# RMSNorm with SiLU on one core: three of four Squares on ScalarE, Silu by whole blocks, and constants and gamma's copy made in small pieces

## The chip, the core and the metric

The kernel runs on one core of a Trainium2 chip. The metric is the device time of one execution in microseconds (us). A single core has no second state to tell apart here: all executions but one (in e6) count as fast, and all have a granted clock of 1.0. The times of experiments are given as a ratio to the kernel before, run in the same rounds on the same chip, with a 95% interval. A ratio is the record's own figure, from fast runs of the same rounds, so it is not quite the ratio of the medians that are quoted, nor of the means of all listed runs. The span of a trace is about 1.8 us shorter than the device time of the same execution (316.25 against 318.03 for the profiled run of before).

## The reference

```python
x: (8, 1024, 2048) float32, gamma: (2048,), eps = 1e-5
rms = sqrt(mean(x**2, axis=-1, keepdims=True) + eps)
out = gamma * x / rms
return out * (1 / (1 + exp(-out)))          # SiLU
```

67.1 MB are read and 67.1 MB written, with a handful of operations on each element.

## The kernel before

The 8192 rows are cut into 16 blocks of 128 partitions by 4 rows (4 MB each). Six blocks are in flight. A block is loaded by SyncE's queue; its four sums of squares are split between VectorE and ScalarE; VectorE scales it by 1/rms and gamma; ScalarE does Silu in place and issues the store. The next load into the buffer waits for that store.

```python
def sums(b, after_first=()):
    na = J // 2                                  # J = 4 rows
    for j in range(na, J):
        nc.vector.tensor_tensor_reduce(out=junk_v, in0=row(b, j), in1=row(b, j), ..., accum_out=ss[:, j:j + 1])
    for j in range(na):
        nc.scalar.activation(out=junk_a, in_=row(b, j), func=ACT.Square, accum_out=ss[:, j:j + 1])
        if j == 0:
            for s in after_first:
                store(s)                         # store of an older block, issued behind the first Square
    ...                                          # Sqrt on ScalarE gives rms
def finish(b, halves=False):
    for j in range(J):
        nc.vector.scalar_tensor_tensor(...)      # row * rstd * gamma
        if j % 2:
            ...                                  # Silu on two rows at a time
...
        nc.vector.memset(ones, 1.0)              # 128 x 128
        ...                                      # gamma is spread by matmul with ones into PSUM
        nc.vector.tensor_copy(out=g, in_=junk_v) # 128 x 2048
        ...
        for b in range(1, last - 1):
            sums(b + 1, after_first=[b - 1])
            finish(b)
            invert(b + 1)
```

So the store of block b-1 stands on ScalarE's queue behind the first Square of block b+1, and with it behind the landing of load b+1.

## Time and profile before

| | before |
|---|---|
| device time, median of 6 | 317.48 us (317.27 to 317.81) |
| span of the profiled run | 316.3 us |
| bytes moved by DMA | 134.2 MB, 424 GB/s over the span |
| busy, VectorE and ScalarE | 71% and 71% |
| first store issued | 36.67 us |
| last half store issued / landed | 304.8 / 315.3 us |

The profile's main lines and how to read them are in the prediction below. Two views of it became important only afterwards. The first is the end of the run in 1 us windows (columns: window, length, busy time of PE, PEld, DVE, ACT, POOL with counts, PE clock, share of the 16 DMA engines, GB/s):

```profile
312.00:313.00 1.00, 0.00 (x0) 0.00 (x0) 0.00 (x0) 0.00 (x0) 0.00 (x0) 1.00 1.03 442
313.00:314.00 1.00, 0.00 (x0) 0.00 (x0) 0.00 (x0) 0.00 (x0) 0.00 (x0) 1.00 0.24 98
314.00:315.00 1.00, 0.00 (x0) 0.00 (x0) 0.00 (x0) 0.00 (x0) 0.00 (x0) 1.00 0.04 16
315.00:316.00 1.00, 0.00 (x0) 0.00 (x0) 0.00 (x0) 0.00 (x0) 0.00 (x0) 1.00 0.00 0
```

One DMA engine of 16 is a share of 0.0625. So the 16 engines do not finish together: most are done soon after 313, and one or two work on to 314.9. The second is in the page's list of DMA queues, with packets, MB and share of 16 engines' span:

```profile
q1 hardware_dynamic: 2304, 67.11, 49.7%
...
q14 instruction: 3, 0.02, 0.0%
```

Queue q1 carries the loads. Queue q14 carries the program itself: three packets of 8192 bytes in this run.

### The profile page before, as it was taken

What the parts mean: (1) busy time and instruction counts of PE and PEld (TensorE: products, weight loads), DVE (VectorE), ACT (ScalarE), POOL (GpSimd) and SP (SyncE); (2) the same over time, 40 slices, a digit from 0 to 9 for tenths busy, and PEclk for the clock granted to TensorE, in tenths of its full rate; (3) what the DMA queues carried; (4) which work ended last, traced back from release to release, by engine and by line L of the source; (5) the groups of instructions that cost most, each with busy time, mean ns of one, the idle gap of its engine ahead of it and who ended that gap; (6) DMA issues with size and microseconds to landing.
All of it is one profiled execution on the core that took longest, in us unless ns stands there. A gap on an engine that the chain in (4) does not pass through costs nothing.

```text
span 316.3 us, 444 instructions
## 1 busy us (share of the span) xinstructions
PE 2.1 (1%) x8; PEld 0.5 (0%) x8; DVE 223.5 (71%) x147; ACT 223.8 (71%) x144; POOL 0.2 (0%) x4
## 2 busy tenths in 40 slices
PE   0200000000000000000000000000000000000000
PEld 0000000000000000000000000000000000000000
DVE  0679499999493983939849397593966939993900
ACT  1357958999967777678676687676786776879540
POOL 0000000000000000000000000000000000000000
DMA  8999999999999999999999999999999999999996
GB/s 328 402 464 410 452 390 410 452 419 443 439 424 452 411 452 410 452 414 456 406 456 414 448 414 448 439 423 452 414 452 410 452 414 456 406 456 410 452 407 269
DMA packets 4763, 134.25 MB, mean 425 GB/s; under 512 B 532, under 2 KB 532, under 8 KB 536
## 3 DMA queue, kind: packets, MB, share of 16 engines
q1 hardware_dynamic: 2304, 67.11, 49.7%
q10 hardware_dynamic: 2456, 67.12, 49.2%
q14 instruction: 3, 0.02, 0.0%
HBM read 67.12 MB, written 67.11 MB: 424 GB/s over the span
## 4 chain that ended last, share of the span: by engine, by line
DMA 74%; DVE 14%; ACT 5%; issue 2%; DVEq 1%; ACTq 0%; SPq 0%
DMA xt<-in_x_dram 44%; DMA out_dram<-xt 30%; DVE xt L84 11%; ACT xt L88 3%; DVE junk_v L64 3%; ACT junk_a L68 1%; DVEq L164 1%; ACT L74 0%; ACT rms L74 0%; DVE rstd L79 0%; ACTq L93 0%; DVE ss L64 0%; SPq L52 0%; DVEq L64 0%; ACTq L74 0%
## 5 line engine op out<-in xcount | busy, mean ns | idle before, releaser
L84 DVE SCALAR_TENSOR_TENSOR xt<-xt,rstd,g 128x2048 f32<-128x2048 f32 x64 | 146.2, 2347 | 0.1
L88 ACT ACTIVATE xt<-xt 128x4096 f32<-128x4096 f32 x32 | 115.4, 3615 | 36.8 <-DVE xt L84 36.7
L64 DVE CUSTOM_DVE_ANT_0 junk_v<-xt 128x2048 f32<-128x2048 f32 x32 | 73.5, 2298 | 56.1 <-DMA xt<-in_x_dram 55.5
L68 ACT ACTIVATE junk_a<-xt 128x2048 f32<-128x2048 f32 x32 | 60.1, 1879 | 29.2 <-DMA xt<-in_x_dram 28.3
L74 ACT ACT_TABLE_LOAD x15 | 19.2, 1283 | 9.9 <-DVE ss L64 9.9
L88 ACT ACT_TABLE_LOAD x15 | 19.2, 1283 | 3.1 <-DVE xt L84 2.9
L79 DVE RECIPROCAL rstd<-rms 128x4 f32<-128x4 f32 x16 | 2.8, 172 | 11.3 <-ACT rms L74 11.3
L114 DVE COPY g<-junk_v 128x2048 f32<-128x2048 f32 x1 | 2.3, 2292 | 9.2 <-PE junk_v L112 9.2
L68 ACT ACTIVATION_READ_ACCUMULATOR junk_a<-xt 128x1 f32 x32 | 6.0, 186 | 0.0
L74 ACT ACTIVATE rms<-ss,eps_t 128x4 f32<-128x4 f32 x16 | 4.8, 297 | 1.2 <-DVE ss L64 1.1
L64 DVE DVE_READ_ACCUMULATOR2_ANT ss<- 128x1 f32 x32 | 4.5, 141 | 0.0
L112 PE MATMUL junk_v<-xt,ones 1*128 1x512 f32 x8 | 2.1, 1133 | 8.1 <-DMA xt<-in_gamma_dram 8.1
L107 ACT ACT_TABLE_LOAD x1 | 1.3, 1283 | 0.7 <-PEq L150 0.7
L105 DVE MEMSET ones<- 128x128 f32 x1 | 0.2, 165 | 0.8 <-PEq L150 0.8
L112 PEld LDWEIGHTS junk_v<-xt,ones 1*128 1x128 f32 x8 | 0.5, 306 | 8.1 <-issue 8.1
L107 ACT ACTIVATE junk_a<-ones 128x1 f32<-128x1 f32 x1 | 0.2, 174 | 0.0
L150 POOL MEMSET const-uint8-127<- 128x1 uint8 x1 | 0.1, 102 | 0.0
L150 POOL MEMSET const-bfloat16-1.0<- 128x1 bf16 x1 | 0.1, 101 | 0.0
L150 POOL MEMSET const-float32-0.0<- 128x1 f32 x1 | 0.1, 98 | 0.2 <-issue 0.2
L150 POOL MEMSET const-float32-1.0<- 128x1 f32 x1 | 0.1, 98 | 0.0
L106 DVE MEMSET eps_t<- 128x1 f32 x1 | 0.1, 59 | 0.0
## 6 DMA issues: line engine op xcount, KB each, us to landing
xt<-in_x_dram SPq DMA_DIRECT2D x16, 4096.0 KB, 42.0
out_dram<-xt ACTq DMA_DIRECT2D x15, 4096.0 KB, 35.2
out_dram<-xt ACTq DMA_DIRECT2D x2, 2048.0 KB, 10.4
xt<-in_gamma_dram ACTq DMA_DIRECT2D x1, 8.0 KB
```

Of the source, the lines that this page charges most:

```text
L64: nc.vector.tensor_tensor_reduce(out=junk_v, in0=row(b, j), in1=row(b, j), scale=1.0, scalar=0.0, op0=ALU.mult, op1=ALU.add, accum_out=ss[ ...
L68: nc.scalar.activation(out=junk_a, in_=row(b, j), func=ACT.Square, accum_out=ss[:, j:j + 1])
L74: nc.scalar.activation(out=rms, in_=ss, func=ACT.Sqrt, scale=1.0 / d, bias=eps_t)
L79: nc.vector.reciprocal(out=rstd, in_=rmss.pop(b))
L84: nc.vector.scalar_tensor_tensor(out=row(b, j), in0=row(b, j), scalar=rstds[b][:, j:j + 1], in1=g, op0=ALU.mult, op1=ALU.mult)
L88: nc.scalar.activation(out=blocks[b][:, cols], in_=blocks[b][:, cols], func=ACT.Silu)
L105: nc.vector.memset(ones, 1.0)
L107: nc.scalar.activation(out=junk_a[:, 0:1], in_=ones[:, 0:1], func=ACT.Square)
L112: nc.tensor.matmul(junk_v[:, c * w:(c + 1) * w], ones[k:k + 1, :], grow[k:k + 1, 0:w], start=True, stop=True)
L114: nc.vector.tensor_copy(out=g, in_=junk_v)
L150: nc = _bacc.Bacc("TRN2", target_bir_lowering=False, num_devices=1)
L164: with _tile.TileContext(nc) as tc:
```

## The change

ScalarE squares three of four rows in blocks 2 to 14, so that VectorE, which waits for loads, sums one row; Silu runs once over a whole block (but for the last one), which saves ScalarE instructions. VectorE's constants and gamma's copy are made in 32 + 16 pieces instead of 1 + 1 instructions, 46 instructions more.

```diff
-        na = J // 2
+        na = J - 1 if 2 <= b <= 14 else J // 2
...
-            if j % 2:
-                cols = slice((j - 1) * d, (j + 1) * d)
+            if j % 2 and (halves or j == J - 1):
+                cols = slice((j - 1) * d, (j + 1) * d) if halves else slice(0, J * d)
...
-        nc.vector.memset(ones, 1.0)
+        for c in range(0, P, 4):
+            nc.vector.memset(ones[:, c:c + 4], 1.0)
...
-        nc.vector.tensor_copy(out=g, in_=junk_v)
+        for c in range(0, d, P):
+            nc.vector.tensor_copy(out=g[:, c:c + P], in_=junk_v[:, c:c + P])
```

## The prediction

> **What bounds the kernel now.** I read the page first: the busy tenths in 40 slices, the DMA total and the chain that ended last.
>
> ```profile
> ACT  1357958999967777678676687676786776879540
> DMA  8999999999999999999999999999999999999996
> HBM read 67.12 MB, written 67.11 MB: 424 GB/s over the span
> DMA 74%; DVE 14%; ACT 5%; issue 2%; DVEq 1%; ACTq 0%; SPq 0%
> ```
>
> The reader is to see that the transfers are at nine tenths or more in 38 of 40 slices, while VectorE and ScalarE are busy 71% of the span each, and that three quarters of the chain are transfers. The bytes are fixed: 134.2 MB. Then the groups by line, which price every instruction that the change touches:
>
> ```profile
> L84 DVE SCALAR_TENSOR_TENSOR xt<-xt,rstd,g 128x2048 f32<-128x2048 f32 x64 | 146.2, 2347 | 0.1
> L88 ACT ACTIVATE xt<-xt 128x4096 f32<-128x4096 f32 x32 | 115.4, 3615 | 36.8 <-DVE xt L84 36.7
> L64 DVE CUSTOM_DVE_ANT_0 junk_v<-xt 128x2048 f32<-128x2048 f32 x32 | 73.5, 2298 | 56.1 <-DMA xt<-in_x_dram 55.5
> L68 ACT ACTIVATE junk_a<-xt 128x2048 f32<-128x2048 f32 x32 | 60.1, 1879 | 29.2 <-DMA xt<-in_x_dram 28.3
> L114 DVE COPY g<-junk_v 128x2048 f32<-128x2048 f32 x1 | 2.3, 2292 | 9.2 <-PE junk_v L112 9.2
> L105 DVE MEMSET ones<- 128x128 f32 x1 | 0.2, 165 | 0.8 <-PEq L150 0.8
> ```
>
> Both engines wait for loads of x (55.5 us and 28.3 us). ScalarE's other wait, 36.7 us, is Silu waiting for VectorE's scaling. Third, the timeline of one steady block (columns: start, us, engine, line, what, then the idle time before it and its releaser):
>
> ```profile
> 84.02 1.88 ACT L68 ACTIVATE junk_a<-xt 128x2048 f32<-128x2048 f32 x1 [0.29 <-DMA xt<-in_x_dram]
> ...
> 88.74 9.13 DVE L84 SCALAR_TENSOR_TENSOR xt<-xt,rstd,g 128x2048 f32<-128x2048 f32 x4
> ...
> 97.91 3.62 ACT L88 ACTIVATE xt<-xt 128x4096 f32<-128x4096 f32 x1 [0.91 <-DVE xt L84]
> 103.39 1.88 ACT L68 ACTIVATE junk_a<-xt 128x2048 f32<-128x2048 f32 x1 [1.86 <-DMA xt<-in_x_dram]
> 103.45 0.34 ACTq L93 DMA_DIRECT2D out_dram<-xt  x1
> ```
>
> A load lands at 84.0; VectorE sums two rows, scales the block before it until 97.9; Silu's second half ends at 101.5; the next load lands 1.86 us later, and only then, behind the first Square of the new block, is the store issued. So per block the compute chain takes 17.5 us of a period of 19.4 us. (From 142.73 to 258.88 us there are six periods of 19.36 us: 8.39 MB in 19.36 us is 433 GB/s.) Fourth, the table of 4 us windows over the end; the last two columns are the DMA share and GB/s:
>
> ```profile
> 300.00:304.00 4.00, 0.00 (x0) 0.00 (x0) 1.09 (x1) 3.09 (x2) 0.00 (x0) 1.00 0.89 385
> 304.00:308.00 4.00, 0.00 (x0) 0.00 (x0) 0.00 (x0) 0.74 (x1) 0.00 (x0) 1.00 1.01 432
> 308.00:312.00 4.00, 0.00 (x0) 0.00 (x0) 0.00 (x0) 0.00 (x0) 0.00 (x0) 1.00 0.99 422
> 312.00:316.00 4.00, 0.00 (x0) 0.00 (x0) 0.00 (x0) 0.00 (x0) 0.00 (x0) 1.00 0.33 139
> ```
>
> Even in the tail the transfers do not run dry: the last two half stores are issued at 300.25 and 304.77, and data flows until about 313.3 (a third of the last window). The chain view puts VectorE and ScalarE on the path there, but the queue still held older stores.
>
> **What the Trainium skill says.** "DMA: Bandwidth & Descriptors", section Where 436 GB/s comes from, gives a ceiling of 435 GB/s for the 16 DMA engines of a core; 433 GB/s in the steady part agrees, so nothing is left to gain there. The same page, section Queues, rings and completion order, says that each DMA engine goes round the queues that have work. The windows agree as far as they go: with loads alone (4 to 36 us) the mean is 428 GB/s, and in the stores-only 304 to 312 us it is 427. So it matters whether any queue has bytes, not which. "ScalarE: Activation LUTs", section What ACT_TABLE_LOAD costs, gives 186 ns plus 0.833 ns an element, and 1283 ns a table load; the trace has 3617 ns for 4096 elements (the formula says 3598) and 1283 ns. "VectorE: DVE Perf Modes", section The TRN2 errata, says that many small pieces pay a fixed cost each, 120 cycles at 0.96 GHz when the source is PSUM; the trace before has no such piece.
>
> **The change part by part.** *Square.* For blocks 2 to 14, 13 row sums go from VectorE to ScalarE. From the timeline, one more Square with its accumulator read costs ScalarE 2.03 us (84.02 to 86.05), and one row sum fewer saves VectorE 2.39 us (84.13 to 86.52). Over the run this is +26 us on ScalarE and -31 us on VectorE.
>
> *Silu by blocks.* One 8192-element Silu is, from 3617 ns for 4096 and 0.833 ns for each further element, 7.03 us; two halves back to back take 7.12. It removes 15 instructions but only 0.1 us a block. What it costs is latency: Silu starts after the fourth scaled row, not the second.
>
> *Steady block.* New chain from a load's landing: 0.11 to VectorE's start, 2.39 for one row sum, 9.14 for four scalings, 0.03 handoff, 7.03 Silu: 18.7 us instead of 17.5. The period set by the transfers is 19.36 us, so 0.7 us of slack is left out of 1.86. ScalarE's own work per block is 3 x 2.03 + 1.28 + 0.30 + 1.28 + 7.03 = 16.0 us with its gaps, VectorE's 2.4 + 9.1 + 0.2 = 11.7: both below 19.36. Steady cost: zero.
>
> *Constants.* 32 memsets of 4 columns: the memset of one column took 59 ns, so about 32 x 60 ns = 1.9 us, from 0.8 to 2.8 us. ScalarE's warm-up reads column 0 alone, and dependencies here go by regions (before, the first Silu half starts after two of four rows), so gamma's load, issued at 1.03, keeps its place. The matmuls need all pieces, but start at 8.1. Cost zero.
>
> *Gamma's copy.* One copy took 2.29 us, from 10.24 to 12.5. A piece of 128 columns is 133 ns of data plus, by the skill's figure, 125 ns: 16 x 258 ns = 4.1 us (an estimate from that page), so it ends at about 14.4. VectorE's first row sum began at 13.24 when load 0 had landed: block 0 starts 1.1 us late.
>
> *Start-up.* Block 0's scaling then ends at 30.2, the whole Silu at 37.2 (before 32.7), the two Squares of block 1 at 41.2: store 0 is issued at 41.3 instead of 36.67. Until the backlog of landed loads is worked off, ScalarE is the bound at 16.0 us a block where the kernel before needed 14 (55.81, 69.78, 84.08). Stepping on: store 1 at 61.6 (was 55.8), store 2 at 77.6 (69.8), store 3 at 93.6 (84.1), store 4 at 109.6 (103.4), and then it catches up, since 16.0 is below 19.4. Does the DMA run dry? By 41.3 some 16.8 MB have moved, of 25.2 MB of loads issued. By 77.6 some 33 MB, of 37.7 issued even before store 2. By 109.6 some 47 MB, of about 54. There are always 4 MB or more queued, so delays of 5 to 10 us in issuing are absorbed. Cost zero.
>
> *Tail.* From the landing of load 14 (258.88): store 13 at +18.7 (was +17.5), store 14 at +28.0 (was +26.8), and all that follows 1.2 us later, so the last stores go out at 301.4 and 306.0. From 304.77 to 313.3 the DMA moved about 3.66 MB, of which 2.10 are the last half store: 1.56 MB, or 3.6 us, were queued ahead. A delay of 1.2 us is under that. At 300.25 it is 1.4 MB, or 3.3 us. Cost zero, with 2 us in reserve.
>
> **Sum:** 0 to 0.3 us; I predict 317.6 us.
>
> **Rivals.** (a) *ScalarE becomes the bound.* For it: Silu ends only 0.7 us before the next load, and ScalarE's busy share goes from 71% to about 79%. Against it: 16.0 us of work in 19.36, and VectorE need not wait for ScalarE to begin on a landed block. A load 1 us early would delay one store by less than 1 us, and two stores and two loads are in flight at a time (35 and 42 us to landing at 19.4 us a block). At worst the chain paced every block; even 1 us over on 12 blocks would give 329, but 18.7 does not reach 19.36. (b) *The tail runs dry.* If the start-up lag never closes, or the loads land later by s, the last store is late by 1.2 + s. Beyond 3.3 us each microsecond adds one: a lag of 5 us would give about 320. For it: stores 2 and 3 are 8 to 10 us late. Against it: late stores leave the DMA to the loads, so loads land earlier, not later. (c) *Gain:* VectorE loses 31 us of work and ScalarE 15 instructions. Where computing bound, it would show; here VectorE's saved 2.4 us a block only shortens a part of a chain that the longer Silu lengthens again. With the bytes fixed I see at most 0.5 us: 317. (d) The small pieces delay the start: at most 2 us, in front of a queue of 12 MB of loads; hidden.
>
> **Range and chances.** Fixed bytes at the ceiling hold the bottom at about 316.5. The top is rival (b) in a mild form, or a slightly different mix of loads and stores: 319.5. More than 2% faster (below 311.0) would need more than the DMA ceiling: 0.01. More than 2% slower (above 323.7) needs rival (a) or a large (b): 0.05. Within 2%: 0.94.
>
> **What would show it.** After the change I expect DMA at nine tenths in all but the end slices; 8192-element Silus of about 7.03 us; DVE busy down by about 28 us to 196 and ACT up by about 25 to 249; the copies of gamma lasting 3 to 4.2 us in all; the first store at about 41 us; in steady state idle time on ScalarE before the first Square of about 0.7 us, still released by the load; the last store at about 306. It would be wrong if the steady period grew, if windows below 390 GB/s appeared in the middle or before the last stores, or if stores were released by ScalarE throughout rather than by landed loads.

## The result

| | before | after |
|---|---|---|
| median of 6 | 317.48 us (317.27 to 317.81) | 318.92 us (317.79 to 319.30) |
| ratio of fast runs | | 1.0042 (1.0026 to 1.0059) |
| first store issued | 36.67 us | 40.47 us |
| last half store issued | 304.77 us | 303.76 us |
| last half store landed | 315.3 us | 316.6 us |

The issue of the first store in the two timelines, before and after:

```profile
36.67 0.36 ACTq L93 DMA_DIRECT2D out_dram<-xt  x1
40.47 0.36 ACTq L94 DMA_DIRECT2D out_dram<-xt  x1
```

About 1.3 us slower: within 2%, inside the range, above the 317.6 us foretold. The page of the changed kernel (busy tenths in 40 slices, the instruction queue, the bytes, the chain by engine):

```profile
ACT  1352994999999999997896868968689786797620
DMA  8999999999999999999999999999999999999994
...
q14 instruction: 4, 0.03, 0.0%
HBM read 67.12 MB, written 67.11 MB: 423 GB/s over the span
DMA 49%; ACT 22%; DVE 17%; issue 7%; DVEq 1%; PE 1%; ACTq 0%; SPq 0%
```

The DMA is as full as before. The chain now follows ScalarE through the start-up, which it did not before, but that is only the backlog described in the prediction: no transfer waits for it. The groups by line:

```profile
L85 DVE SCALAR_TENSOR_TENSOR xt<-xt,rstd,g 128x2048 f32<-128x2048 f32 x64 | 146.2, 2348 | 0.1
L69 ACT ACTIVATE junk_a<-xt 128x2048 f32<-128x2048 f32 x45 | 84.5, 1878 | 18.3 <-DMA xt<-in_x_dram 16.7
L65 DVE CUSTOM_DVE_ANT_0 junk_v<-xt 128x2048 f32<-128x2048 f32 x19 | 43.7, 2298 | 60.9 <-DMA xt<-in_x_dram 60.8
L117 DVE COPY g<-junk_v 128x128 f32<-128x128 f32 x16 | 3.3, 281 | 8.6 <-PE junk_v L114 8.6
L107 DVE MEMSET ones<- 128x4 f32 x32 | 0.9, 62 | 0.8 <-PEq L153 0.8
```

The 13 moved Squares, the unchanged scaling and the 48 pieces are all there; their durations are compared with the prediction below. A steady block in the timeline:

```profile
159.09 1.88 ACT L69 ACTIVATE junk_a<-xt 128x2048 f32<-128x2048 f32 x1 [0.91 <-DMA xt<-in_x_dram]
...
161.41 9.13 DVE L85 SCALAR_TENSOR_TENSOR xt<-xt,rstd,g 128x2048 f32<-128x2048 f32 x4
...
170.58 7.03 ACT L89 ACTIVATE xt<-xt 128x8192 f32<-128x8192 f32 x1 [2.51 <-DVE xt L85]
178.58 1.88 ACT L69 ACTIVATE junk_a<-xt 128x2048 f32<-128x2048 f32 x1 [0.97 <-DMA xt<-in_x_dram]
178.64 0.34 ACTq L94 DMA_DIRECT2D out_dram<-xt  x1
```

Period 19.5 us, Silu done at 177.61, and ScalarE still waits 0.97 us for the load, which also releases the store. So nothing is lost in the steady part. Nor in the last stores, which were issued 1.0 us *earlier* than before. Yet the last one landed 1.3 us later. The 1 us windows of the changed kernel's end show where:

```profile
313.00:314.00 1.00, 0.00 (x0) 0.00 (x0) 0.00 (x0) 0.00 (x0) 0.00 (x0) 1.00 0.39 164
314.00:315.00 1.00, 0.00 (x0) 0.00 (x0) 0.00 (x0) 0.00 (x0) 0.00 (x0) 1.00 0.08 33
315.00:316.00 1.00, 0.00 (x0) 0.00 (x0) 0.00 (x0) 0.00 (x0) 0.00 (x0) 1.00 0.04 16
```

The bulk ends within half a microsecond of before, and then a share of one engine in 16 works on for two microseconds. The trace holds, for each transfer, 16 completion marks, taken here as one for each DMA engine. Those of the last half store, on the clock of the span (the expectations below quote the trace's own clock, which is 11.1 us ahead):

```
             1st      15th     16th
before     313.46    314.46   315.33 us
after      313.70    314.65   316.59 us
```

Fifteen engines are 0.2 us later than before, the sixteenth 1.3 us. **The whole loss is one straggling DMA engine.** It was late early on: of the second load, the sixteenth mark came 0.85 us after the fifteenth, where before it was 0.15. Between these two loads lies the one thing that was not there before, an instruction packet at 17.4 us. The times of the instruction packets after the start are 93.6, 108.7 and 304.7 us in the kernel before, and 17.4, 98.0, 289.6 and 296.1 us after.

### The profile page after: what moved, and what is told of

It reads as the page before. It is cut to its first block, busy times and chain, and to the rows that moved or that the text cites. A ratio compares the mean times of both kernels' runs of the same rounds, so it can differ in the third digit from the quotient of the medians.

```text
span 317.5 us, 484 instructions
## 1 busy us (share of the span) xinstructions
PE 2.1 (1%) x8; PEld 0.5 (0%) x8; DVE 195.0 (61%) x167; ACT 246.6 (78%) x155; POOL 0.2 (0%) x4
## 3 DMA queue, kind: packets, MB, share of 16 engines
q1 hardware_dynamic: 2304, 67.11, 49.5%
## 4 chain that ended last, share of the span: by engine, by line
DMA 49%; ACT 22%; DVE 17%; issue 7%; DVEq 1%; PE 1%; ACTq 0%; SPq 0%
DMA out_dram<-xt 24%; DMA xt<-in_x_dram 23%; ACT xt L89 14%; DVE xt L85 13%; ACT junk_a L69 4%; DMA xt<-in_gamma_dram 2%; DVE junk_v L65 2%; ACT L75 2%; ACT L89 1%; DVE g L117 1%; DVEq L167 1%; PE junk_v L114 1%; ACT rms L75 0%; DVE rstd L80 0%; DVE ss L65 0%
## 5 line engine op out<-in xcount | busy, mean ns | idle before, releaser
L89 ACT ACTIVATE xt<-xt 128x8192 f32<-128x8192 f32 (+1 forms) x17 | 112.7, 6628 | 36.1 <-DVE xt L85 36.0
L69 ACT ACTIVATE junk_a<-xt 128x2048 f32<-128x2048 f32 x45 | 84.5, 1878 | 18.3 <-DMA xt<-in_x_dram 16.7
L65 DVE CUSTOM_DVE_ANT_0 junk_v<-xt 128x2048 f32<-128x2048 f32 x19 | 43.7, 2298 | 60.9 <-DMA xt<-in_x_dram 60.8
L117 DVE COPY g<-junk_v 128x128 f32<-128x128 f32 x16 | 3.3, 281 | 8.6 <-PE junk_v L114 8.6
L69 ACT ACTIVATION_READ_ACCUMULATOR junk_a<-xt 128x1 f32 x45 | 8.4, 186 | 0.0
L65 DVE DVE_READ_ACCUMULATOR2_ANT ss<- 128x1 f32 x19 | 2.7, 142 | 0.0
L107 DVE MEMSET ones<- 128x4 f32 x32 | 0.9, 62 | 0.8 <-PEq L153 0.8
```

Of the source, the lines that this page charges most:

```text
L89: nc.scalar.activation(out=blocks[b][:, cols], in_=blocks[b][:, cols], func=ACT.Silu)
L107: nc.vector.memset(ones[:, c:c + 4], 1.0)
L117: nc.vector.tensor_copy(out=g[:, c:c + P], in_=junk_v[:, c:c + P])
```

## The experiments

Two things were read from the traces of all runs besides the views above. *Fetches* are the instruction packets after the start. *Slow loads* are load packets of 32 KB begun after 50 us that took over 1240 ns, where nearly all take 1213; the figure behind them is their extra time summed over the 16 engines (16 us of it is 1 us of every engine). Packets carry no engine's number, but each engine's packets follow one another within some 5 ns, so they can be sorted into 16 chains; where two chains are in step the sorting is ambiguous. (The 241 slow packets and 72 us that the expectation of e4 quotes for e2 count from 41 us on; 216 of them begin after 50 us.) One profiled execution each:

```
                    first store   slow loads      last store's marks        fetches
                    issued        n, extra us     1st     15th    16th      (us)
before              36.7            2,  0.8      313.46  314.46  315.33     93.6 108.7 304.7
changed kernel      40.5            4,  0.6      313.70  314.65  316.59     17.4 98.0 289.6 296.1
e1_pieces           37.1            2,  0.8      313.33  314.66  315.44     18.4 95.4 264.6 304.1
e2_square_silu      40.0          216, 58.6      315.36  319.47  319.47     96.7 126.6 290.8
e3_pool_pad         37.0            8,  2.7      315.46  316.22  318.70     11 of them
e4_work_half0       36.5           14,  3.7      313.30  314.96  315.03     92.8 128.3 282.2
e5_whole0           40.0          170, 38.5      315.10  318.86  319.30     94.0 104.6 305.5
e6_after_half0      37.1            1,  0.2      313.63  315.13  315.31     18.4 95.6 281.3 297.2
e7_store0_late      40.1          211, 65.0      316.43  319.63  319.64     89.3 104.5 305.6
e8_store0_43        43.3            2,  0.8      313.40  314.37  315.20     89.9 103.8 298.6
e9_work_memsets     39.9          174, 51.1      315.65  318.61  319.06     52.1 97.3 293.0
e10_work_copies     40.4           13,  2.7      313.60  315.03  315.96     88.2 97.9 288.3
e11_pool_memsets    40.4           37,  5.5      313.49  314.93  316.60     88.2 97.8 289.4
```

The first theory, F: the fetch of VectorE's instructions takes turns with the data on one DMA engine, that engine never catches up, and the pieces bring such a fetch forward and add another. Its rival, W: the loss is in the work, the late stores of the start-up and the longer Silu.

### e0: the changed kernel again

No edit.

> The changed kernel once more, as the base for the others. In its trace one of the 16 DMA engines ended about 2.5 us after the other 15 (landings of the last store: fifteenth at 325.78, sixteenth at 327.72 on the trace's clock; kernel before 325.59 and 326.45). All theories: +1.0 to +1.6 us against before, and the same late last landing.

Median 318.94 us (318.12 to 319.32), ratio 1.0043 (1.0031 to 1.0055). Its fetches came at 17.7, 97.7, 288.1 and 294.9 us, and its last marks were 313.37, 314.40 and 316.61: the same straggler. Its first store went out at 40.78 us and its trace has no slow load (as defined above) at all, so this loss does not need slow loads.

### e1: the small pieces alone

```diff
 (kernel before)
-        nc.vector.memset(ones, 1.0)
+        for c in range(0, P, 4): nc.vector.memset(ones[:, c:c + 4], 1.0)
-        nc.vector.tensor_copy(out=g, in_=junk_v)
+        for c in range(0, d, P): nc.vector.tensor_copy(out=g[:, c:c + P], in_=junk_v[:, c:c + P])
```

> The kernel before with the 47 small pieces alone. Theory F (fetch): the loss is a DMA engine that fetches VectorE's instructions, 0.3 us of packet and up to 0.9 us in all each time; the 46 extra instructions bring its first fetch from 108.7 to about 17 us and add one near the end. Then this kernel loses most of the 1.3 us: +0.8 to +1.5 us, the instruction queue shows 4 packets or more, and the last landing is again 1.5 us or more after the fifteenth. Rival W (work): the loss is the late stores of the start-up and the longer Silu; then this kernel is within 0.3 us of before.

Median 319.05 us, ratio 1.0054 (1.0035 to 1.0072). The pieces alone (48 of them; the expectation miscounts by one) cost 1.7 us, and W alone cannot be right. The executions fall in two groups, 318.1 to 318.5 and 319.6 to 319.9. The profiled one was of the faster group, so the last mark was only 0.8 us behind the fifteenth, not the 1.5 us expected. But this trace is the cleanest for the mechanism. One chain of 256 packets' worth of data has a gap at each of VectorE's two fetches, and a slow packet behind it:

```
fetch at 18.4 us:   gap 302 ns, next 32 KB packet +560 ns
fetch at 264.6 us:  gap 302 ns, next 32 KB packet +532 ns
sum 1.70 us; this chain's last packet ended at 315.07 us, the bulk of the others at 313.4
```

The fetch packet itself takes 309 ns. What each costs the engine is 0.8 to 0.9 us here, and the engine carries that to the end: every chain holds about 256 packets' worth of data, so the others did not take over any of its share.

### e2: Square and Silu alone

```diff
 (changed kernel)
-        for c in range(0, P, 4): nc.vector.memset(ones[:, c:c + 4], 1.0)
+        nc.vector.memset(ones, 1.0)
-        for c in range(0, d, P): nc.vector.tensor_copy(out=g[:, c:c + P], in_=junk_v[:, c:c + P])
+        nc.vector.tensor_copy(out=g, in_=junk_v)
```

> The changed kernel without its small pieces: Square and Silu as changed, constants and copy as before. Theory F: within 0.4 us of before, since VectorE now has 26 instructions fewer than before and its fetch comes later, not earlier; the instruction queue shows 3 packets or fewer. Rival W: +1.0 to +1.5 us, as the changed kernel.

Median 321.33 us (319.33 to 322.71), ratio 1.0116 (1.0088 to 1.0145). Both theories missed: the changed kernel *without* its small pieces is 3.7 us slower than before, and slower than with them. The fetch came at 126.6 us as F says, and there is no lone straggler. From the page, the loads' queue and the total:

```profile
q1 hardware_dynamic: 2304, 67.11, 50.1%
...
HBM read 67.12 MB, written 67.11 MB: 419 GB/s over the span
```

The same 2304 packets took 50.1% of 320.4 us, 160.5 us, where before they took 49.7% of 316.3 us, 157.2 us: 3.3 us more on the average engine. And the end in 1 us windows:

```profile
315.00:316.00 1.00, 0.00 (x0) 0.00 (x0) 0.00 (x0) 0.00 (x0) 0.00 (x0) 1.00 0.76 328
316.00:317.00 1.00, 0.00 (x0) 0.00 (x0) 0.00 (x0) 0.00 (x0) 0.00 (x0) 1.00 0.61 262
317.00:318.00 1.00, 0.00 (x0) 0.00 (x0) 0.00 (x0) 0.00 (x0) 0.00 (x0) 1.00 0.42 180
```

Here many engines are late, by different amounts. The trace has 216 slow loads, in clusters of 10 to 30 once a block (62 to 66 us, 82 to 86, 102 to 106, and so on). So there is a second cost, of another kind, which the pieces hide in the changed kernel.

### e3: useless instructions on an idle engine

```diff
 (kernel before)
+        for _ in range(1024):
+            nc.gpsimd.memset(pad, 0.0)          # pad: a 128 x 1 tile that nobody reads
```

> The kernel before with 1024 one-column memsets on GpSimd, which is idle otherwise; nothing waits for them. They do no work that matters, but the instructions have to be fetched: at 128 instructions of 64 bytes to a packet of 8192 bytes about 8 packets more. Theory F: if they all lie on one DMA engine, that engine falls behind by 8 times 0.3 to 0.9 us, and the kernel ends +2.4 to +7 us later. If fetches are free, or taken up by slack: within 0.3 us of before.

Median 321.86 us (321.47 to 321.96), ratio 1.0135 (1.0122 to 1.0148): +4.3 us for work that nothing waits for. The page:

```profile
POOL 6666666666666666666610000000000000000000
...
q14 instruction: 11, 0.09, 0.1%
```

Eleven packets where the kernel before had three; the eight of GpSimd come when 76, 203, 335, ... 973 of its instructions are recorded, some 128 apart. Each has the same gap of 0.30 us, with +0.22 to +0.35 us on the packet behind it; the eight sum to 5.0 us. From 166 to 282 us, the sixteenth mark of each load comes 4.7 to 4.8 us after the fifteenth. All eight therefore lay on one DMA engine. The last load is late by that engine's lag, the compute of the last blocks with it, and between 303.5 and 305.4 us the other 15 engines stand empty for 0.7 to 1.9 us. The instructions of VectorE and ScalarE lasted as long as before (scaling 2347 ns, Silu 3615 ns), so the memsets did not slow those. F's mechanism is shown, at larger size.

### e4: Square and Silu alone, with block 0 in halves

The question now is what makes loads slow in e2. The clusters start with the first stores, and the first store goes out at 40.0 us where before it went out at 36.7, because block 0's Silu is whole. Theory P: where in a load the first store begins sets how loads and stores interleave from then on. Rival W: the whole-block Silu and the Squares in every block do it.

```diff
 (e2)
-            if j % 2 and (halves or j == J - 1):
-                cols = slice((j - 1) * d, (j + 1) * d) if halves else slice(0, J * d)
+            if j % 2 and (halves or b == 0 or j == J - 1):
+                cols = slice((j - 1) * d, (j + 1) * d) if halves or b == 0 else slice(0, J * d)
```

> The kernel with Square and Silu changed but no small pieces lost 3.7 us, and its trace shows another loss than a fetch: 241 packets of loads of 32 KB took over 1240 ns where nearly all take 1213, 72 us of extra packet time on 16 engines. This kernel is the same, but block 0 does Silu in two halves as before, so that the first store goes out at about 36.7 us instead of 40.0. Theory P (phase): how loads and stores interleave is set by where in a load the first store starts, and the slow packets come from the first store at 40.0; then this kernel is within 0.5 us of before, with fewer than 60 slow load packets. Rival W (work): the slow packets come from the whole-block Silu and the three Squares in every block; then it stays at +2.5 us or more.

Median 317.64 us (317.38 to 317.74), ratio 1.0000 (0.9988 to 1.0011), first store at 36.5 us, 14 slow loads. W falls: the 13 moved Squares and 14 whole Silus cost nothing. All of e2's 3.7 us came from block 0.

### e5: block 0's whole Silu alone

```diff
 (kernel before)
-            if j % 2:
-                cols = slice((j - 1) * d, (j + 1) * d)
+            if j % 2 and (b or j == J - 1):
+                cols = slice((j - 1) * d, (j + 1) * d) if b else slice(0, J * d)
```

> The kernel before with the whole-block Silu in block 0 alone; all other blocks as before. The first store goes out at about 40.0 us. Theory P: +2 to +4 us and some 200 slow load packets, though 15 of 16 blocks are as before. Rival W: within 0.3 us of before.

Median 321.57 us, ratio 1.0118 (1.0103 to 1.0133). One Silu of 16 done in one piece instead of two costs 3.8 us.

### e6: the changed kernel with block 0 in halves

The edit of e4, made to the changed kernel.

> The changed kernel (small pieces too) with Silu in halves in block 0 alone: first store at about 37 us. Theory P with F: only the fetch loss remains, so about as the small pieces alone: +0.8 to +1.7 us, no more slow load packets than before outside 36 to 46 us. Rival W: as the changed kernel or worse, with its slow packets on one engine each block.

Median 318.82 us, ratio 1.0031 (1.0009 to 1.0053); one of its six executions (322.55 us) is over 1.5% above its fastest and does not count as fast. Against e4 it differs only in the pieces: they cost about 1.0 us here. As foretold, though in this profiled execution, again one of the faster ones, the straggler is hardly seen.

### e7: the first store 3.4 us later, nothing else

```diff
 (kernel before)
-            if j == 0:
+            if j == (1 if b == 2 else 0):
                 for s in after_first:
                     store(s)
```

> The kernel before with one move: the first store is issued behind block 2's second Square, not its first, so at about 40.2 us instead of 36.7. No computing changes. Theory P: +2 to +4 us with some 200 slow load packets. Rivals: within 0.3 us, since stores issued 5 to 10 us late are absorbed by queued transfers.

Median 321.54 us, ratio 1.0129 (1.0110 to 1.0149), 211 slow loads. The issue of the first store in the timeline:

```profile
40.09 0.35 ACTq L93 DMA_DIRECT2D out_dram<-xt  x1
```

No computing was changed at all. Moving one DMA issue from 36.67 to 40.09 us costs 4.1 us.

### e8: the first store 6.7 us later

```diff
 (kernel before)
-            if j == 0:
+            if j == 0 and b != 2:
                 for s in after_first:
                     store(s)
...
         rmss[b] = rms
+        if b == 2:
+            for s in after_first:
+                store(s)
```

> The kernel before with its first store later still: behind block 2's square root, at about 43.2 us instead of 36.7. At 40.0 to 40.2 us, 2 us before load 3 has landed (42.2), three kernels lost 3.7 to 4.1 us. Theory P (phase of the first store within a load, period 9.7 us): 43.2 us is 1 us into load 4, so the loss falls to 1.5 us or less, with fewer than 100 slow load packets. Rival L (lateness): each microsecond of delay of the first store costs about one, so +5 us or more.

```profile
43.34 0.35 ACTq L96 DMA_DIRECT2D out_dram<-xt  x1
```

Median 317.40 us, ratio 0.9993 (0.9981 to 1.0006), 2 slow loads. Later still, and nothing is lost. So it is not lateness but the place: 36.7, 40.5 and 43.3 us are good or nearly so, and 39.9 to 40.1 us is bad.

What makes the place bad is not shown. Load 3 (counted from 0) landed at 42.0 to 42.2 us in the four bad runs (e2, e5, e7, e9), but also at 42.1 us in e10, which is good. The first store's packets begin about 4 us after its issue, behind packets of load 4. By the sorted chains, some engines begin it behind two packets of load 4 and the others behind three. In the bad runs the 16 engines are divided over the two: 11 and 5 in e2, 8 and 8 in e5, 10 and 6 in e7, 11 and 5 in e9. In the good runs near them nearly all are alike: 3 and 13 in e10, 2 and 14 in the changed kernel. Engines out of step at the first store thus go with slow loads; no run changes this alone. (In e11 it is 6 and 10, with 37 slow loads.)

### e9: e2 with the memset pieces

```diff
 (e2)
-        nc.vector.memset(ones, 1.0)
+        for c in range(0, P, 4): nc.vector.memset(ones[:, c:c + 4], 1.0)
```

> Square and Silu as changed with the 32 memset pieces, but gamma copied in one. The first store stays at about 40.0 us; VectorE's first instruction fetch comes early (at about 35 us or before), and sets one DMA engine back. The changed kernel (+1.3 us) has both the early fetch and a first store 0.5 us later (40.5), and lost less than the same work without the pieces (+3.7). If the early fetch breaks the slow packets: +0.8 to +2 us here. If the 0.5 us did it: +3 us or more here.

Median 321.83 us (319.13 to 323.31), ratio 1.0122 (1.0085 to 1.0160): as bad as e2. The fetch came earlier, at 52.1 us, but not as early as 35, so this run alone leaves open what a fetch at 17 us would do. The next one settles it.

### e10: e2 with the copy pieces

```diff
 (e2)
-        nc.vector.tensor_copy(out=g, in_=junk_v)
+        for c in range(0, d, P): nc.vector.tensor_copy(out=g[:, c:c + P], in_=junk_v[:, c:c + P])
```

> Square and Silu as changed with gamma's copy in 16 pieces, but one memset. The first store comes at about 40.5 us as in the changed kernel; VectorE has 15 instructions more and its first fetch comes near 85 us, not at 17. If the 0.5 us of the first store broke the slow packets: +0.3 to +1.5 us here, with fewer than 60 slow load packets. If the early fetch did it: +3 us or more here.

Median 317.60 us (317.16 to 318.67), ratio 0.9997 (0.9979 to 1.0015), 13 slow loads. Sixteen copies instead of one make the kernel 3.7 us *faster* than e2, because they are slower: 1 us more of VectorE's time holds block 0 back, and the first store goes out at 40.43 instead of 39.97 us. The two issues, e2 above e10:

```profile
39.97 0.35 ACTq L94 DMA_DIRECT2D out_dram<-xt  x1
40.43 0.36 ACTq L94 DMA_DIRECT2D out_dram<-xt  x1
```

This is the changed kernel less its memset pieces, so the changed kernel's 1.3 us come from those 32 memsets. Not every execution of e10 is free of loss: three took 317.2 us and three 318.0 to 318.7.

### e11: the memset pieces on GpSimd

```diff
 (changed kernel)
-            nc.vector.memset(ones[:, c:c + 4], 1.0)
+            nc.gpsimd.memset(ones[:, c:c + 4], 1.0)
```

> The changed kernel with its 32 memset pieces moved from VectorE to GpSimd; nothing else. The same number of small instructions runs at the same place, but VectorE's instruction count is again that of the kernel with copies alone (ratio 0.9997), and GpSimd with 40 instructions stays short of the about 65 at which an engine's first fetch was seen. Theory F: 3 packets in the instruction queue, none before 80 us, and within 0.3 us of before. Rival: the pieces cost by their number or by what they do to the matmuls and gamma's copy; then +1.0 us or more, as the changed kernel.

Median 318.03 us (317.56 to 319.37), ratio 1.0017 (1.0000 to 1.0034). Three fetches, the first at 88.2 us, as F says; the time lies between F's and the rival's figure, and the interval touches that of e0 and overlaps that of e10. The ratio says +0.5 us; the means of all six listed runs and of the 11 of before differ by 0.8 us. Four executions were at 317.6 to 318.3 and two at 319.3 to 319.4. The profiled one was of the two. It has no extra fetch, but 37 slow loads with 5.5 us of extra time, 1.9 us of it on the chain that ended last. So fetches are not the only thing that makes a straggler: with a first store at 40.4 us, half a microsecond from the bad place, some executions lose on one engine what e2 loses on all.

## Why the prediction was right, and which step was wrong

**What bounds the kernel: right.** DMA stayed at nine tenths in all slices but the first and last, and e4 shows that the main part of the change, Square and Silu in all blocks but block 0, is worth nothing either way (1.0000).

**Steady block: right.** The Silu took 7.03 us as worked out. From the landing at 159.09 to the Silu's end at 177.61 are 18.5 us (18.7 foretold), with 0.97 us left on ScalarE (0.7 foretold). VectorE's busy time is 195.0 us (196 foretold), ScalarE's 246.6 (249).

**Start-up: the times right, the conclusion too simple.** Stores 0 to 4 went out at 40.5, 60.6, 76.6, 92.5 and 108.4 us (41.3, 61.6, 77.6, 93.6 and 109.6 foretold). "Cost zero" held in the changed kernel, and e8 shows that a store 6.7 us late can be free. But the reason given, that queued bytes absorb any delay, is not the whole of it: at 40.0 us, with the same bytes queued, the same delay costs 3.7 to 4.1 us (e2, e5, e7). The prediction was saved by 0.46 us that gamma's copy added.

**Constants: this is the step that failed.** "Cost zero" looked at VectorE's time alone, and there it was right: the 32 memsets took 0.9 us, half of the 1.9 foretold (each lasts 62 ns as expected, but they overlap), and nobody waited. The term that was left out is their fetch. The pieces add 46 instructions to VectorE and the moved row sums take 26 away; the fetch that came at 108.7 us came at 17.4, and one more at 296.1. In the changed kernel's trace these two account for 0.87 and 0.66 us of gap and slow packet. Some ten slow packets of about 0.1 us each, nearly one a block, on what the sorting takes for the same engine, make up about 1.0 us more; whether the fetch brings them about is not shown. Together that is 2.5 us, and the last engine did end 2.4 to 2.8 us after the bulk (316.2 against 313.4 to 313.8). Without the memset pieces the loss is gone (e10, 0.9997); with them on GpSimd it is 0.5 to 0.8 us instead of 1.3 (e11). The fetches themselves are shown to cost time by e1 and, eight of them at once, by e3; that they are all of the memsets' loss in the changed kernel is not.

**Gamma's copy: size off, sign as foretold.** It took 3.26 us, not 4.1. A piece lasts 281 ns, not 258, but the pieces overlap and start 199 ns apart, so block 0's first row sum on VectorE began 0.4 us late, not 1.1.

**Tail: right for the wrong engine count.** The last stores went out even earlier than foretold (303.76 against 306.0), because load 14 landed 2.3 us earlier than before, as rival (b) argued. The tail did not run dry. But the working read the end of the data, 313.3 us, from the mean share of 16 engines, while the last of them worked to 314.9; and it took the DMA for one server with 1.56 MB queued. It is 16, and a queue that is full on average says nothing of the engine that is furthest behind.

**Sum and range: held by luck.** The sum of 0 to 0.3 us left out the term that cost 1.3 us. The measured 318.92 us lies under the top of 319.5 us, but that top was set for a mild tail loss or another mix of loads and stores, not for a fetch; with gamma's copy in one piece (e9) the first store went out 0.6 us earlier and the time was 321.8 us, above that top.

**What stays open.** Why loads are slow when the first store goes out at 40.0 us, and why they stay so for the rest of the run, is not shown; only that the place of one DMA issue switches it. Nor is it shown what puts an execution of e1, e6, e10 or e11 in the faster or the slower of its groups. So the split of the changed kernel's 1.3 us between the two fetches and its nearness to the bad place is known only roughly, from e11: 0.5 to 0.8 us for either. That split rests on one run whose interval touches those of e0 and e10. None of the variants beats the kernel before: the best three (e4, e8, e10) are equal to it.

## What to carry to other kernels

When all 16 DMA engines are full to the end, as here, the time is that of the most delayed one: look at the spread of a transfer's completion marks, not only at the mean share, and count small instructions on any engine, even an idle one, as fetches that one DMA engine pays for. Before crediting or blaming a change of some microseconds in such a kernel, move the first store alone by a few microseconds, as in e7 and e8: here that was worth 4 us, three times the effect under study.

## What the Trainium skill lacked or had wrong

- "Runtime: NRT & Kernel Launch", section Instruction fetch mechanics, says that instructions are fetched ahead in 16 KiB blocks by the engine's own DMA queue and calls the cost of crossing a block "mostly hidden". In these traces no compute engine was seen to wait for one. But the packets seen were 8192 bytes, 128 instructions apart on GpSimd, and each that was followed by a data packet set one DMA engine back by 0.4 to 0.9 us in the traces read for it (before, changed kernel, e1, e3); eight of them made the kernel 4.3 us slower (e3).
- "DMA: Bandwidth & Descriptors", section Queues, rings and completion order, describes the turn-taking between queues on each engine, and the prediction took from it that only queued bytes matter. No page says that the place of the first store within a load can make some 200 of 2048 load packets up to 1.0 us slower; the runs show +4.1 us at 40.1 us (e7) and nothing at 36.7 or 43.3 us.
- "VectorE: DVE Perf Modes", section The TRN2 errata, gives 120 cycles, 125 ns, of fixed cost for PSUM to SBUF. With 133 ns for 128 columns that gives 258 ns a piece (an estimate from that page); a piece lasted 281 ns. But sixteen of them took 3.26 us in all: with 281 ns for the last that is 199 ns from start to start, 66 ns beyond the 133 ns of data, since they overlap.
- "DMA: Bandwidth & Descriptors", section Specifications, gives about 27 GiB/s for one DMA engine. A packet of 32768 bytes took 1213 ns, which is 27.0 GB/s (25.2 GiB/s), and 16 such engines give 432 GB/s, against 433 GB/s in the steady part.
